# Row sums by accumulating DMAs among the heads, and another order of transfers and units around the gate's stage, in a hybrid attention trunk on one core

## The chip, the core and the metric

The kernel runs on one core of a Trainium2 chip. The core has five engines, each with its own in-order queue: TensorE (PE in the profile, with its weight loads as PEld), VectorE (DVE), ScalarE (ACT), GpSimd (POOL) and SyncE (SP), which only issues DMAs. POOL issues DMAs too; in this kernel those that add to what lies in memory are issued by POOL. All transfers run on the core's 16 DMA engines. The metric is the device time of one launch in microseconds (us); the median of three runs counts.

## The reference

One layer of a decoder trunk on 1024 tokens of width 2048, all in f32. Shortened:

```python
hn = rmsnorm(h, norm_mix_g)
sb_q, sb_k, sb_v, sb_g, df_q, df_k, df_v, df_g = split(hn @ w_in)      # 8 x 1024 columns
sb_out = stick_breaking_attention(sb_q, sb_k, sb_v)                    # 8 heads of 128
df_out = rmsnorm(differential_attention(rope(df_q), rope(df_k), df_v, lam), subln_g)   # 8 heads of 128
mixed = concat([sb_out * silu(sb_g), df_out * silu(df_g)])
h = h + mixed @ w_out
gate = sigmoid(rmsnorm(h, norm_ple_g) @ w_ple_gate)
h = h + gate * (p @ w_ple_proj)                                        # p: 1024 x 256
return rmsnorm(h, norm_final_g)
```

## The kernel before, in words

**Tiles.** Everything is kept transposed: a tile has 128 features as partitions and a half of the tokens (`HALF` = 512) along the free axis. Half 1 holds the later 512 tokens and is worked on first, then half 0. Each f32 operand of a product is split into a high and a low part, and a product is three matmuls: high by high (L213), high by low (L214) and low by high (L215). A `unit` is 96 such matmuls of 128x512 that give two feature blocks of 128; it takes its weights from `Stream` in four chunks of 512 KB. For each chunk SP loads `wraw` (L150), ACT makes `whi` (L151), DVE makes `wlo` (L152).

**Stages.** First come the 16 heads for half 1 (the trace's first 800 us): eight stick-breaking heads (0 to 7), then eight differential ones (8 to 15). Then come the 16 heads for half 0 (to about 1750 us): `ORDER0` begins with the differential heads 8 to 15 and ends with the stick-breaking ones. A head is two units and, interleaved with the matmuls of the next units by `Side`, its attention. At its end DVE has the gated result of the head, `sg`, and SP stores it to `mixed_d` in memory (L410). For half 0 POOL loads the keys and values of half 1 back (`k2`, `kl`, `v2`, L571 to L575). The sum of squares of half 0's input, which half 0's norm needs, is taken at head 8 of half 1: sixteen tiles `xs` are loaded (SP, L585), squared (ACT, L109) and added (POOL, L110), all at once.

**The out-projection** is one level of a Strassen-like scheme (seven products in place of eight). Its four quadrants are A11, A12 (half 1) and A21, A22 (half 0); each product works on a quadrant or on a sum of quadrants: S1 = A21 + A22, S2 = S1 - A11, S3 = A21 - A11, S4 = A12 - S2. `combine` makes these sums for a pair of heads, eight times: SP loads four tiles `cmb` (L246), POOL does four additions of 128x512 (L249 to L252), and SP stores four tiles to `comb_d` (L254). It is called among the heads of half 0, and the last time inside the out-projection. The products then run for 16 pairs (ph, u). Each gets its result tile `hc` from DVE, and POOL puts it to memory: a plain store to `half_d` in ph 0, an accumulating DMA into `h_d` in ph 1 (`put`, L744 and L746). In this stage the order on DVE and ACT is the order in the code (`manual_schedule`).

**The gate's stage** (from about 2060 us) begins with the last pair (1, 7) of the out-projection. Loads of the normalised operand (`xl`, L910 to L914), of the embedding (`praw`, which gives `ph` and `pl`, L655 to L657) and of its weights (`pw`, giving `pwh` and `pwl`, L665 to L669) stand between the last products, whose results are `hc` of L939 and L993. Then come eight gate units for half 1 and eight for half 0. The first two are held back, `acc0` in `acc` banks and `acc1` in a `za` tile, until the norm's `rstd` is there, which needs the sixteen tiles of the residual loaded (`load_h`) and squared; these stand in one burst behind the first unit. `ple` (12 matmuls, L677 to L679) multiplies the embedding by `pwh` and `pwl` into `pls`; `gated` multiplies by the gate and adds. For unit u from 2 on the order is `ple(1, u)`, `plew(1, u + 1)`, unit, `gated(1, u)`. There is one `ph` and one `pl`, rewritten for half 0 by `embedding(0)`; this stands behind `ple(1, 7)` and ahead of the last unit of half 1.

**The tail.** The last unit of half 0 is done in two quarters of 256 tokens (`tq`). Behind each, DVE does the gate (L1116 to L1119), a square (L1121), PE sums it over the partitions (`ssps`, L1122), `rstd_from` (L90 to L94) gives `r`, and `final` multiplies the tiles by it (L623, L626) and SP stores the output. POOL does the multiplications for tq 0 and the first ones for tq 1.

Of the kernel before, what the change touches and what calls it, by code (L numbers as in the profile page):

```python
# [13 lines left out]
F32 = mybir.dt.float32  # L14
# [6 lines left out]
P = 128  # L21
# [7 lines left out]
ORDER1 = [*range(16)]  # L29
ORDER0 = [*range(8, 16), 0, 4, 1, 5, 2, 6, 3, 7]  # L30
EPS = 1e-6
# [15 lines left out]
def _body(ctx, nc, tc, ap):  # L47
# [95 lines left out]

    def wprep(wsrc, pc, by_halves=False):
        raw = wp.tile([P, 2, 2, 2, P], F32, name="wraw", tag="wraw", bufs=2)
        hi = wp.tile([P, 2, 2, 2, P], F32R, name="whi", tag="whi")
        lo = wp.tile([P, 2, 2, 2, P], F32R, name="wlo", tag="wlo")

        def part(o):
            lastw[0] = nc.sync.dma_start(raw[:, o], wsrc[pc][:, o])  # L150
            A.copy(hi[:, o], raw[:, o])  # L151
            V.tensor_tensor(lo[:, o], raw[:, o], hi[:, o].bitcast(F32), op=ALU.subtract)  # L152

        part(slice(0, 1 if by_halves else 2))
        return hi, lo, partial(part, slice(1, 2))

    class Stream:
# [6 lines left out]
        def gates(self):  # L164
            units = [ap["w_gate"][u] for _ in range(2) for u in range(8)]
            self.todo = deque((w, pc) for w in units[:-1] for pc in range(4))
            self.prep()

        def prep(self, by_halves=False):
            hi, lo, second = wprep(*self.todo.popleft(), by_halves=by_halves)  # L170
            self.ready.append((hi, lo))
            return second
# [58 lines left out]

    def combine(ph, i):

        a, b = KA[ph][i]
        if lastput[0] is not None:
            with tc.issue_after(lastput[0].ins):
                return combine_(ph, i, a, b)
        return combine_(ph, i, a, b)

    lastput = [None]  # L240

    def combine_(ph, i, a, b):
        t = []
        for src in (mixed_d[0, a], mixed_d[0, b], mixed_d[1, a], mixed_d[1, b]):
            x = ev.tile([P, HALF], F32, name="cmb", tag="xt", bufs=4)
            nc.sync.dma_start(x, src)  # L246
            t.append(x)
        a21, a22, a11, a12 = t
        G.tensor_tensor(a22, a21, a22, op=ALU.add)  # L249
        G.tensor_tensor(a21, a21, a11, op=ALU.subtract)  # L250
        G.tensor_tensor(a11, a22, a11, op=ALU.subtract)
        G.tensor_tensor(a12, a12, a11, op=ALU.subtract)  # L252
        for j, x in enumerate((a22, a11, a21, a12)):
            nc.sync.dma_start(comb_d[ph, j, i], x)  # L254


    def attention(at, pz, half, hd, q, qz, K, KL, VV, sg, vf):
# [102 lines left out]
        def mix(pr, g):  # L360
# [25 lines left out]
            if sb:  # L386
                V.tensor_tensor(sg[:, ms_], av, sg[:, ms_], op=ALU.mult)
                if pr == 1:
                    nc.sync.dma_start(mixed_d[half, hd], sg)
                return  # L390
# [9 lines left out]
        def norm(pr):  # L400
# [8 lines left out]
            if pr == 1:  # L409
                nc.sync.dma_start(mixed_d[half, hd], sg)  # L410

# [22 lines left out]
    with tc.tile_pool(name="at", bufs=2) as at, tc.tile_pool(name="pz", bufs=2, space=PSUM) as pz:  # L434
# [4 lines left out]
        for half in (1, 0):  # L439
# [34 lines left out]
            for hd in (ORDER0, ORDER1)[half]:  # L474
# [103 lines left out]
                side.add(attention(at, pz, half, hd, q, qz, K, KL, VV, sg, vf))  # L578
                if half == 1 and hd == H:
                    pin = lastw[0].ins  # L580
                    ss0 = SumSq(ev, "ssq")
# [12 lines left out]
                if half == 0 and hd < H and hd:  # L594
                    n = ORDER0.index(hd) - H
                    combine(*((0, n - 1) if n < 5 else (1, n - 5)))

# [53 lines left out]

        def embedding(half):
            for k in range(2):
                praw = ev.tile([P, HALF], F32, name="praw", tag="xt", bufs=4)
                nc.sync.dma_start(praw, ap["pT"][k * P:(k + 1) * P, half * HALF:half * HALF + HALF])  # L655
                A.copy(ph[:, k, :], praw)
                V.tensor_tensor(pl[:, k, :], praw, ph[:, k, :].bitcast(F32), op=ALU.subtract)  # L657
# [3 lines left out]
        plws = {}  # L661

        def plew(half, u):
            wr = ev.tile([P, 2, 2, P], F32, name="pw", tag="xt", bufs=4)
            nc.sync.dma_start(wr, ap["w_pp"][u])  # L665
            wh = at.tile([P, 2, 2, P], F32R, name="pwh", tag="awh")
            wl = at.tile([P, 2, 2, P], F32R, name="pwl", tag="awl")
            A.copy(wh, wr)
            V.tensor_tensor(wl, wr, wh.bitcast(F32), op=ALU.subtract)  # L669
            plws[half, u] = wh, wl  # L670

        def ple(half, u):
            wh, wl = plws.pop((half, u))
            z = pz.tile([P, 2, HALF], F32, name="ple", tag="z")
            for c in range(2):
                for k in range(2):
                    T.matmul(z[:, c, :], wh[:, k, c, :], ph[:, k, :], start=k == 0, stop=False)  # L677
                    T.matmul(z[:, c, :], wh[:, k, c, :], pl[:, k, :], start=False, stop=False)
                    T.matmul(z[:, c, :], wl[:, k, c, :], ph[:, k, :], start=False, stop=k == 1)  # L679
            pls = pair("pls", "st")  # L680
            A.copy(pls, z)
# [59 lines left out]
        def put(o, ph, hf, ch):  # L741

            if ph:
                lastput[0] = G.dma_start(h_d[hf, ch], o, accum_op=ALU.add)  # L744
            else:
                lastput[0] = G.dma_start(half_d[hf, ch], o)  # L746

# [106 lines left out]
        def whigh():  # L854
# [8 lines left out]
            else:  # L863
                t = at.tile([P, 2, 4 * P], F32R, name="wpr", tag=tag, bufs=BUFS.get(tag, 2))
            A.copy(t[:, 0], src)  # L865
            wmade.append((src, t))

        def wlow():
# [6 lines left out]
            wmade[i] = None  # L875
            V.tensor_tensor(t[:, 1], src, t[:, 0].bitcast(F32), op=ALU.subtract)
            ph, u = UNITS[n]
# [64 lines left out]
        for ph in range(2):  # L942
            for u in range(8):
                last = ph == 1 and u == 7
                r = {}
                for e in ((1, u), (1, u + 8), (0, u), (0, u + 8)) if ph else ():
                    r[e] = ev.tile([P, HALF], F32, name="hr", tag="xt", bufs=4)
                    nc.sync.dma_start(r[e], half_d[e])
# [17 lines left out]
                if ph:  # L966
                    V.tensor_tensor(u2, u2, r[1, u + 8], op=ALU.add)

                def p2():
# [25 lines left out]
                if ph:  # L995
                    V.tensor_tensor(s1, s1, r[0, u], op=ALU.add)
                if last:
                    p2()
                prev = u, ph, b, c, s1, u2
                if ph == 0 and u == 1:  # L1000
                    combine(1, 3)
                if ph == 0 and 1 <= u < 5:
# [3 lines left out]
        pl = pair("pl", "v", F32R)  # L1006
        embedding(1)
# [6 lines left out]
        while xq and len(xq) > 8:  # L1014
            xq.popleft()[1]()

        last_ = [None, None]
        X = GX
        ple(1, 0)
        ple(1, 1)  # L1020
        for _ in range(len(xq) - 4):
            xq.popleft()[1]()
        plew(1, 2)
        s2 = SumSq(ev, "ssq")

        def xrest():
            while xq:
                xq.popleft()[1]()

        acc0 = unit(X, mid={2: xrest})  # L1030
        man2.__exit__(None, None, None)
        ss1 = SumSq(ev, "rstd1")
        for u in range(8):
            load_h(1, u)
            for c in range(2):
                ss1.add(h[1, u + 8 * c])
        za = pz.tile([P, 2, HALF], F32, name="za", tag="z")
        rs = []
        acc1 = unit(X, acc=[za[:, 0, :], za[:, 1, :]], mid={3: lambda: rs.append(ss1.rstd(ev, "rstd0"))})
        rstd = rs[0]  # L1040
        ss0 = SumSq(ev, "rstd1")
        gated(1, 0, acc0, rstd)
        gated(1, 1, acc1, rstd)
        for u in range(2, 8):
            ple(1, u)
            if u < 7:
                plew(1, u + 1)
            else:
                embedding(0)
                plew(0, 0)  # L1050
            acc = unit(X)
            for v in ((0, 1), (2, 3), (4,), (5,), (6,), (7,))[u - 2]:
                load_h(0, v)
# [45 lines left out]
        for tq in range(2):  # L1099
# [13 lines left out]
            for c in range(2):  # L1113
# [7 lines left out]
                V.tensor_tensor(s, t, t, op=ALU.mult)  # L1121
# [65 lines left out]
```

## Time and profile before

| | us |
|---|---|
| runs | 2513.76, 2515.78, 2515.96 (median 2515.78) |
| profiled execution, time | 2510.27 |
| profiled execution, span | 2508.5 |
| PE busy | 2441.4 (97%) |
| DVE, ACT, POOL busy | 1668.4, 1161.9, 288.9 |

A span is the time from the first to the last instruction of the profiled execution. In a window of 50 us PE is busy all 50.00 us where nothing holds it up. Matmuls overlap: each row of a 128x512 matmul is 0.39 us long, while the next starts 0.23 us later, so a stall that the profile shows as x us of idle time costs x + 0.16 us. A granted clock below 1.00 is a stretch in which TensorE ran slower.

### The profile page before, as it was taken

The numbers are of one execution on the slowest core, as the hardware profiler recorded it, in microseconds if no ns is written. First come the engines' busy times: TensorE is split into PE (matmuls) and PEld (weight loads), VectorE is DVE, ScalarE is ACT, GpSimd is POOL, SyncE is SP. The second block draws the span as 40 slices with busy tenths as digits, with TensorE's granted clock in tenths as the row PEclk, the third lists the DMA queues.
The fourth block names the chain that finished last, engine by engine and source line by source line (L and its number), as shares of the span: only waits on it lengthen the run. The fifth ranks groups of instructions, "written<-read, shape, count | busy, mean of one in ns | idle before, by whom it ended". The sixth has DMA issues, their size and how long they took to land.

```text
span 2508.5 us, 31234 instructions
## 1 busy us (share of the span) xinstructions
PE 2441.4 (97%) x11626; PEld 2034.8 (81%) x11626; DVE 1668.4 (67%) x2677; ACT 1161.9 (46%) x1920; POOL 288.9 (12%) x281
## 2 busy tenths in 40 slices
PE   8999999999999999999999999999999998999996
PEld 7888888788887888888887888887787876888886
DVE  6554555777877888888876565667678673547555
ACT  6332333555556655555555333335523224637342
POOL 3000000300000000001111010101021114321112
PEclk9999999999999999999999999999999999999998
DMA  5333333633334333334443333435656786333433
GB/s 189 113 116 116 114 105 125 206 123 118 109 122 164 121 107 122 114 117 143 148 142 126 101 126 94 135 113 183 228 190 217 164 199 211 129 119 115 133 101 101
DMA packets 135415, 346.26 MB, mean 138 GB/s; under 512 B 14496, under 2 KB 18592, under 8 KB 135264
## 3 DMA queue, kind: packets, MB, share of 16 engines
q1 hardware_dynamic: 114096, 288.43, 35.6%
q0 software_dynamic: 21168, 55.85, 7.8%
q8 instruction: 91, 1.49, 0.2%
q14 instruction: 60, 0.49, 0.1%
HBM read 281.31 MB, written 71.30 MB: 141 GB/s over the span
## 4 chain that ended last, share of the span: by engine, by line
PE 87%; DVE 7%; DMA 2%; ACT 2%; issue 1%; SPq 0%; DVEq 0%; ACTq 0%
PE acc L213 20%; PE acc L214 20%; PE acc L215 20%; PE tp L345 2%; PE pbc L756 2%; PE pbc L758 2%; PE pbc L757 2%; DVE st L306 1%; PE z L286 1%; PE z L287 1%; PE av L378 1%; DVE wlo L152 1%; PE av L377 1%; PE av L376 1%; PE pa L758 1%
## 5 line engine op out<-in xcount | busy, mean ns | idle before, releaser
L213 PE MATMUL acc<-xh,whi 128*128 128x512 f32 x2464 | 981.4, 398 | 6.3 <-ACT xh L138 6.3
L214 PE MATMUL acc<-xl,whi 128*128 128x512 f32 x2464 | 963.9, 391 | 0.8 <-DVE xl L139 0.8
L215 PE MATMUL acc<-xh,wlo 128*128 128x512 f32 x2464 | 964.0, 391 | 0.0
L152 DVE TENSOR_TENSOR wlo<-wraw,whi 128x1024 fp32r<-128x1024 f32 (+1 forms) x317 | 398.8, 1258 | 374.5 <-ACT whi L151 369.2
L215 PEld LDWEIGHTS acc<-xh,wlo 128*128 128x128 f32 x2464 | 463.6, 188 | 101.1 <-DVE wlo L152 1.3
L151 ACT CAST whi<-wraw 128x1024 fp32r<-128x1024 f32 (+1 forms) x317 | 333.0, 1051 | 457.2 <-PE acc L214 397.0
L213 PEld LDWEIGHTS acc<-xh,whi 128*128 128x128 f32 x2464 | 464.8, 189 | 93.6 <-ACT xh L138 6.8
L214 PEld LDWEIGHTS acc<-xl,whi 128*128 128x128 f32 x2464 | 464.9, 189 | 88.3 <-DVE xl L139 2.3
L357 ACT CAST awh<-tp 128x256 fp32r<-128x256 f32 (+1 forms) x160 | 80.3, 502 | 180.9 <-PE tp L345 153.5
L358 DVE TENSOR_TENSOR awl<-tp,awh 128x256 fp32r<-128x256 f32 (+1 forms) x160 | 93.1, 582 | 97.9 <-ACT awh L357 96.7
L110 POOL TENSOR_TENSOR ssq<-ssq,sq 128x512 f32<-128x512 f32 x80 | 119.0, 1488 | 326.6 <-ACT sq L109 278.8
L314 ACT ACTIVATE et<-z,mx 128x512 f32<-128x512 f32 (+7 forms) x128 | 94.6, 739 | 53.6 <-DVE mx L311 52.7
L865 ACT CAST wpr<-T 128x512 fp32r<-128x512 f32 x64 | 39.2, 623 | 164.9 <-DVE T L822 164.0
L306 DVE TENSOR_TENSOR_SCAN st<-pt 128x511 f32<-128x511 f32 (+3 forms) x64 | 89.9, 1405 | 20.8 <-ACT pt L304 20.2
L311 DVE TENSOR_REDUCE mx<-z 128x1 f32<-128x512 f32 (+7 forms) x128 | 96.4, 753 | 1.2
L304 ACT ACTIVATE pt<-z 128x512 f32<-128x512 f32 (+3 forms) x64 | 41.6, 650 | 79.7 <-DVE z L293 79.7
L378 PE MATMUL av<-awl,v 128*128 128x256 f32 x256 | 73.4, 287 | 5.2 <-DVE awl L358 5.2
L376 PE MATMUL av<-awh,v 128*128 128x256 f32 x256 | 72.5, 283 | 0.7 <-ACT awh L357 0.7
L377 PE MATMUL av<-awh,v 128*128 128x256 f32 x256 | 72.3, 283 | 0.0
L286 PE MATMUL z<-k,q 128*128 128x512 f32 (+2 forms) x160 | 56.9, 360 | 4.5 <-ACT et L314 4.5
L322 DVE SCALAR_TENSOR_TENSOR et<-et,l 128x512 f32<-128x512 f32 (+3 forms) x64 | 53.0, 829 | 11.8 <-ACT et L321 11.8
L321 ACT ACTIVATE et<-et,l 128x512 f32<-128x512 f32 (+3 forms) x64 | 49.7, 777 | 17.6 <-DVE l L320 17.1
(309 smaller groups left out, 3627.8 us busy)
## 6 DMA issues: line engine op xcount, KB each, us to landing
wraw<-w_in SPq DMA_DIRECT2D x255, 512.0 KB, 3.6
wraw<-w_gate SPq DMA_DIRECT2D x64, 512.0 KB, 3.6
wraw<-w_out SPq DMA_DIRECT2D x56, 256.0 KB, 3.7
k_d<-k POOLq DMA_DIRECT2D x16, 512.0 KB, 3.9
v_d<-v POOLq DMA_DIRECT2D x16, 512.0 KB, 2.9
mixed_d<-sg SPq DMA_DIRECT2D x32, 256.0 KB, 3.1
k<-k_d POOLq DMA_DIRECT2D x16, 512.0 KB, 3.6
v<-v_d POOLq DMA_DIRECT2D x16, 512.0 KB, 4.4
```

The source lines that it names most:

```text
L110: lastadd[0] = eng.tensor_tensor(self.acc, self.acc, s, op=ALU.add)
L151: A.copy(hi[:, o], raw[:, o])
L152: V.tensor_tensor(lo[:, o], raw[:, o], hi[:, o].bitcast(F32), op=ALU.subtract)
L213: T.matmul(acc[c], hi[:, k2, kh, c, :], xh, start=first, stop=False)
L214: T.matmul(acc[c], hi[:, k2, kh, c, :], xl, start=False, stop=False)
L215: T.matmul(acc[c], lo[:, k2, kh, c, :], xh, start=False, stop=last)
L306: V.tensor_tensor_scan(st[:, off + 1:nkey], pt[:, off:nkey - 1], pt[:, off:nkey - 1], initial=1.0, op0=ALU.mult, op1=ALU.bypass)
L311: V.reduce_max(mx, z[:, vw], axis=AX.X, negate=True)
L314: A.activation(et[:, vw], z[:, vw], AF.Exp, bias=mx[:, 0:1], accum_out=l)
L376: T.matmul(av, vv[:, 0, blk % 4, :], wh, start=blk == 2 * pr + 1, stop=False)
L377: T.matmul(av, vv[:, 1, blk % 4, :], wh, start=False, stop=False)
L378: T.matmul(av, vv[:, 0, blk % 4, :], wl, start=False, stop=last)
```

## The change

1. `combine` is gone. `mixed`, called where a head's result was stored, makes the sums as the heads finish. For half 1 ACT makes a negated copy `neg`; heads 0 to 3 and 8 to 11 store it (SP) as the start of S2, S3 and S4, and heads 4 to 7 and 12 to 15 add it to S4 by an accumulating DMA (POOL). For half 0 each head issues three DMAs on POOL that add its result to sums, and heads 0 to 3 and 8 to 11 store it as the start of S1 (SP). S4 is kept negated, and its weights are negated as they are made. Not stored to `mixed_d` any more: half 0's heads 0 to 3 and 8 to 11. `ORDER0` has heads 0 to 7 in plain order.
2. The sixteen `xs` tiles are loaded and squared four at a time in heads 1 to 4 of half 1.
3. Before the gate's stage: `praw` of half 1 is loaded ahead of the last pair, `pw` of units 0 to 2 within it; the first gate weights are loaded there too, and split behind the A22 product; the order of the four `hr` loads of a pair is changed. The residual is loaded and squared two tiles at a time over the chunks of the first units, and a third unit (`zb`) runs before the first `gated`.
4. For units 3 to 7 of half 1 the order is unit, `ple(1, u)`, `plew(1, u + 1)` (or `embedding(0)`), `gated(1, u)`.
5. In the tail DVE does all multiplications of `final`; those of tq 0 stand inside tq 1, behind its square, and `rstd_from` has a higher priority.

```diff
-    def combine_(ph, i, a, b):
-        t = []
-        for src in (mixed_d[0, a], mixed_d[0, b], mixed_d[1, a], mixed_d[1, b]):
-            x = ev.tile([P, HALF], F32, name="cmb", tag="xt", bufs=4)
-            nc.sync.dma_start(x, src)
...
+    def mixed(half, hd, t):
+        ph, second, i = (0 if hd >= H else 1), hd % H >= 4, hd % 4
+        S1, S2, S3, S4 = [comb_d[ph, j, i] for j in range(4)]
+        if half == 1 or second:
+            nc.sync.dma_start(mixed_d[half, hd], t)
+        if half == 1:
+            n = ev.tile([P, HALF], F32, name="neg", tag="xt", bufs=4)
+            A.activation(n, t, AF.Copy, scale=-1.0)
+            if second:
+                G.dma_start(S4, n, accum_op=ALU.add)
+            else:
+                for d in (S2, S3, S4):
+                    nc.sync.dma_start(d, n)
+            return
+        if second:
+            G.dma_start(S1, t, accum_op=ALU.add)
+        else:
+            nc.sync.dma_start(S1, t)
+            G.dma_start(S3, t, accum_op=ALU.add)
+        G.dma_start(S2, t, accum_op=ALU.add)
+        G.dma_start(S4, t, accum_op=ALU.add)
...
-                if half == 1 and hd == H:
+                if half == 1 and 1 <= hd < 5:
...
-                    for kt in range(NK):
+                    for kt in range(4 * hd - 4, 4 * hd):
...
+                if last:
+                    embedding_load(1, (("rstd0", 1), ("rstd1", 1)))
...
+        embedding()
         plew(1, 0)
-        stream.gates()
         rest_of(prev, True)
+        gate0()
         plew(1, 1)
...
+        acc0 = unit(X, mid={2: xrest, 3: partial(residual, 0)})
+        za = pz.tile([P, 2, HALF], F32, name="za", tag="z")
+        acc1 = unit(X, acc=[za[:, 0, :], za[:, 1, :]], mid={i: partial(residual, i + 1) for i in range(4)})
...
+        zb = pz.tile([P, 2, HALF], F32, name="zb", tag="z")
...
+        acc2 = unit(X, acc=[zb[:, 0, :], zb[:, 1, :]], mid={0: partial(residual, 5), 1: more, 3: norm1})
...
-        for u in range(2, 8):
+        gated(1, 2, acc2, rstd)
+        for u in range(3, 8):
+            acc = unit(X)
             ple(1, u)
             if u < 7:
                 plew(1, u + 1)
             else:
-                embedding(0)
+                embedding_load(0, (("xt", 4), ("xt", 4)))
+                embedding()
                 plew(0, 0)
-            acc = unit(X)
...
+            if tq:
+                final(0, slice(0, Q), r2, range(8))
...
-            rstd_from(ms, 1.0 / NK, eps6, EPS, r2, r3)
-            if tq == 0:
-                final(0, ts, r2, range(8), eng=G)
-            else:
-                final(0, ts, r2, (0, 1, 2), eng=G)
-                final(0, ts, r2, (3, 7, 4, 5, 6))
+            with tc.high_priority(offset=400):
+                rstd_from(ms, 1.0 / NK, eps6, EPS, r2, r3)
+        final(0, ts, r2, range(8))
```

More of the change, by code (lines that the diff above doesn't have):

```diff
@@ L650, in load_h, with embedding_load, embedding @@
                 h[half, u + 8 * c] = hc[c]
-        def embedding(half):
+        praws = []
+        def embedding_load(half, tags):
             for k in range(2):
-                praw = ev.tile([P, HALF], F32, name="praw", tag="xt", bufs=4)
+                praw = ev.tile([P, HALF], F32, name="praw", tag=tags[k][0], bufs=tags[k][1])
                 nc.sync.dma_start(praw, ap["pT"][k * P:(k + 1) * P, half * HALF:half * HALF + HALF])
+                praws.append(praw)
+        def embedding():
+            for k in range(2):
+                praw = praws.pop(0)
                 A.copy(ph[:, k, :], praw)
@@ L661, in _body, with plew_load @@
         plws = {}
+        pws = {}
+        def plew_load(half, u):
+            pws[half, u] = ev.tile([P, 2, 2, P], F32, name="pw", tag="xt", bufs=4)
+            nc.sync.dma_start(pws[half, u], ap["w_pp"][u])
         def plew(half, u):
[L664 to L665 removed]
+            if (half, u) not in pws:
+                plew_load(half, u)
+            wr = pws.pop((half, u))
             wh = at.tile([P, 2, 2, P], F32R, name="pwh", tag="awh")
@@ L679, in ple @@
                     T.matmul(z[:, c, :], wl[:, k, c, :], ph[:, k, :], start=False, stop=k == 1)
-            pls = pair("pls", "st")
+            pls = pair("pls", "pt" if half == 1 and u == 2 else "st")
             A.copy(pls, z)
@@ L743, in put @@
             if ph:
-                lastput[0] = G.dma_start(h_d[hf, ch], o, accum_op=ALU.add)
+                G.dma_start(h_d[hf, ch], o, accum_op=ALU.add)
             else:
-                lastput[0] = G.dma_start(half_d[hf, ch], o)
+                G.dma_start(half_d[hf, ch], o)
         def ftile():
```

94 lines of the change are left out of this document (48 added, 46 removed).

## The prediction, made before the changed kernel was run

> **What bounds the kernel now.** I read the page first, then PE's waits, then a table of windows of 50 us, and then the rows around each window in which PE lost time.
>
> ```profile
> PE 2441.4 (97%) x11626; PEld 2034.8 (81%) x11626; DVE 1668.4 (67%) x2677; ACT 1161.9 (46%) x1920; POOL 288.9 (12%) x281
> ```
>
> PE is the bound, 97% busy. The change leaves the matmuls what they were, so only the 67 us in which PE is idle, and slow stretches of its clock, can be won. The windows (columns: window, its length, busy time of PE, PEld, DVE, ACT and POOL, granted clock, DMA share, GB/s) show where these lie:
>
> ```profile
> 100.00:150.00 50.00, 50.00 (x239) 41.88 (x238) 25.48 (x39) 15.86 (x27) 1.23 (x2) 1.00 0.36 111
> 450.00:500.00 50.00, 46.53 (x218) 38.61 (x217) 37.96 (x77) 30.25 (x57) 14.49 (x14) 0.97 0.54 174
> 800.00:850.00 50.00, 47.95 (x217) 39.26 (x216) 40.76 (x86) 29.55 (x59) 1.07 (x2) 0.95 0.46 145
> 1450.00:1500.00 50.00, 47.88 (x233) 39.46 (x233) 33.55 (x39) 18.27 (x28) 10.70 (x6) 1.00 0.42 137
> 1500.00:1550.00 50.00, 50.00 (x256) 42.52 (x256) 31.70 (x39) 19.73 (x28) 1.06 (x2) 1.00 0.33 106
> 2000.00:2050.00 50.00, 50.00 (x222) 41.26 (x221) 32.46 (x51) 10.85 (x19) 8.62 (x10) 1.00 0.74 161
> 2050.00:2100.00 50.00, 42.34 (x179) 34.33 (x178) 33.13 (x49) 22.46 (x34) 6.02 (x7) 0.93 0.86 242
> 2100.00:2150.00 50.00, 47.44 (x199) 38.10 (x199) 22.72 (x24) 30.31 (x43) 25.27 (x18) 0.97 0.45 158
> 2250.00:2300.00 50.00, 50.00 (x220) 41.02 (x220) 35.31 (x44) 34.12 (x49) 8.82 (x6) 1.00 0.36 117
> ```
>
> What PE waited for in three stretches, the first of 1180 to 1280 us and the second of 1460 to 1720, the rest from the whole run (us in total, times, longest):
>
> ```profile
> PE av L378 <- DVE awl L358: 1.9, 2, 0.9
> PE tp L345 <- DVE et L322: 1.2, 2, 0.6
> ...
> PE av L373 <- DVE lead L351: 4.7, 3, 1.6
> PE av L378 <- DVE awl L358: 1.7, 3, 0.6
> ...
> PE pbc L756 <- DVE hc L939: 5.8, 1, 5.8
> PE z L286 <- ACT et L314: 4.5, 2, 3.5
> PE pbc L756 <- DVE hc L993: 2.5, 2, 1.8
> PE za L215 <- DVE wlo L152: 1.5, 1, 1.5
> PE za L213 <- ACT whi L151: 1.1, 1, 1.1
> ```
>
> A stall costs its idle time and 0.16 us more, since rows of matmuls overlap.
>
> **1. Row sums.** Heads with `combine` stall PE, the one between them (1500 to 1550) doesn't. Its POOL additions slow DVE: the same scan and the same difference of a head without `combine` (1405) and one with it (1462):
>
> ```profile
> 1405.32 2.02 DVE L306 TENSOR_TENSOR_SCAN st<-pt 128x895 f32<-128x895 f32 x1
> 1407.44 1.09 DVE L307 TENSOR_TENSOR bt<-st,bt 128x895 f32<-128x895 f32 x1
> ...
> 1462.62 3.11 DVE L306 TENSOR_TENSOR_SCAN st<-pt 128x895 f32<-128x895 f32 x1
> 1463.93 2.88 POOL L251 TENSOR_TENSOR cmb<-cmb 128x512 f32<-128x512 f32 x1
> 1465.84 1.93 DVE L307 TENSOR_TENSOR bt<-st,bt 128x895 f32<-128x895 f32 x1
> ```
>
> That is 1.93 us late on DVE by two instructions, about the 1.6 us of the longest wait for `lead`. The waits of both stretches add up to 1.9 + 1.2 + 4.7 + 1.7 = 9.5 us in 10 waits, so 9.5 + 10 x 0.16 = 11.1 us. All of it goes if POOL does no additions there. What comes instead: 56 accumulating DMAs on POOL; on SP 96 DMAs (32 stores of `sg`, 32 loads, 32 stores of sums) become 56; 16 negated copies on ACT; 32 weight operations with a sign, in place of as many without, at nothing. The nearest rows for an accumulating DMA:
>
> ```profile
> h_d<-hc POOLq DMA_DIRECT2D x32, 256.0 KB, 5.1
> half_d<-hc POOLq DMA_DIRECT2D x32, 256.0 KB, 3.5
> ...
> 2062.47 0.86 POOL L744 DMA_DIRECT2D h_d<-hc  x1 [6.33 <-DVE hc L939]
> 2062.68 0.69 DVE L876 TENSOR_TENSOR wpr<-b,wpr 128x512 fp32r<-128x512 f32 x1
> ```
>
> It lands after 5.1 us, keeps POOL for 0.86 us, and DVE beside it takes its usual 0.69. Three per head of some 58 us are at most 3 x 5.1 = 15 us of all DMA engines, 0.26 of the head on top of 0.33; the window from 2000 ran at 0.74, with such DMAs, and lost nothing. On POOL's queue they stand behind the `k2` and `v2` loads of the next head and half a head ahead of those after it. The copy `neg` is some 0.6 us of an ACT that is 0.3 to 0.6 busy. It stands where SP's store waited for the same `sg`. In these places I take 0; the lower end, no gain at all, is where each collides with weight loads; the upper is 13, with the DVE time of the other `combine`s. Taken: -11 (range -13 to 0).
>
> **2. Squares of half 0's input.** The 3.5 us wait of `z` L286 lies at 453, in the window from 450. ACT stood there for the sixteen tiles and for POOL's additions:
>
> ```profile
> ACT sq L109 <- DMA xs<-xT: 4.7, 4, 1.7
> ACT sq L109 <- POOL ssq L110: 1.0, 3, 0.4
> ```
>
> The stall costs 3.5 + 0.16, and the clock of 0.97 another 0.03 x 50 = 1.5 us: 5.1. In heads 1 to 4 each four tiles meet an ACT that is busy for 16 of 50 us and a DVE for 25 (the window from 100); the price there is between 0 and 1 us.  Taken: -4.5 (range -5 to 0).
>
> **3. Entry to the gate.** The two windows from 2050 lost 7.66 + 2.56 idle and, by their clocks, 3.5 + 1.5 us, 15.9 us with 4 x 0.16. DVE and ACT in order show why `hc` L939 is late, though its product was done:
>
> ```profile
> ACT ph L656 <- DMA praw<-pT: 5.7, 1, 5.7
> ACT pwh L668 <- DMA pw<-w_pp: 2.3, 1, 2.3
> ...
> DVE pwl L669 <- ACT pwh L668: 2.2, 1, 2.2
> DVE pl L657 <- ACT ph L656: 1.4, 1, 1.4
> ```
>
> With `praw` and `pw` loaded early both waits on DMA go, and with them 2.2 + 1.4 + the cast's own time on DVE. I follow DVE's order in the changed kernel: `pl` and `pwl` are still ahead of the addition of L939, so some 1.0 of the 5.8 us stays. The 1.8 us of L993 stays, as the work ahead of it is the same. The waits for `whi` and `wlo` (1.1 and 1.5) came from the burst of squares; with two squares to a chunk of 5.45 us they go. New: the third unit needs the banks of the norm's sum and of `acc` at once; DVE frees them 7.4 us after the sum by my count of its queue, PE arrives after 6.1, so 1.3 us. Left over: 1.8 + 1.0 + 1.3, 3 x 0.16 and some 1 us of clock, 5.6. Taken: -10 (range -14, if only L993 stays, to -2, if the loads, which SP issues one after the other, are late again).
>
> **4. Units 3 to 7.** Here something is lost. `ple(1, 7)` now runs behind the last unit of half 1, and only then may `ph` and `pl` be overwritten; `ple(0, 0)` is the very next on PE. Before, this cast was done 22 us earlier, and the window from 2250 lost nothing:
>
> ```profile
> 2262.45 0.61 ACT L656 CAST ph<-praw 128x512 fp32r<-128x512 f32 x1
> ...
> 2287.34 1.28 ACT L1073 ACT_TABLE_LOAD   x1
> 2289.18 0.60 ACT L668 CAST pwh<-pw 128x512 fp32r<-128x512 f32 x1
> 2289.68 1.01 ACT L681 COPY pls<-ple 128x1024 f32<-128x1024 f32 x1
> ```
>
> From the end of `ple(1, 7)` at about 2287.0: ACT loads its table until 2288.6, then come `ph` of the first half (0.6), `pwh` (0.6), `pls` (1.0) and `ph` of the second (0.6), 2291.4. DVE has `pl`, `pwl`, two products of `gated` that wait for `pls`, 0.69 each, and the second `pl` is there at 2292.9. The fifth matmul of `ple(0, 0)` needs it and would have run at 2287.9: +5.0. In pieces, as the first matmuls go as their parts come. For the clock I take the 0.03 x 50 = 1.5 us of the window from 450, which had a stall of this size; the window from 800 (0.95) shows that pieces slow it as well. Taken: +6 (range +3, if the table load comes earlier, to +8).
>
> TensorE: Matmul & The Clock Gate, section "The HAM clock gate", a page of the Trainium skill, has the clock halve only after about 3.4 us without work. By it a stall in pieces shorter than that costs no clock, and this term would be +5.0; the row of the window from 800 speaks against it, as its 2.05 us of idle time went with a clock of 0.95.
>
> **5. Tail.** Without POOL's `final` DVE is fast again:
>
> ```profile
> 2490.74 1.37 DVE L1121 TENSOR_TENSOR sq<-h 128x256 f32<-128x256 f32 x1
> 2494.84 0.42 DVE L93 SCALAR_TENSOR_TENSOR r<-r,r 128x256 f32<-128x256 f32 x1
> ```
>
> L1119 and L1121 fall from about 1.4 to 0.42 each, four times, 3.9 us; but seven products of tq 0 at 0.69 and two at 0.42 (5.7 us) now stand on DVE in the same stretch, some of it in waits for ACT. Counted through the queue, `r` comes 1.1 us earlier and the last product 1.8 earlier, and a store follows each as before. Taken: -1.8 (range -4 to +1).
>
> **Sum.** -11 - 4.5 - 10 + 6 - 1.8 = -21.3. Against the profiled execution, 2510.27, that gives 2489.0; the median of the runs is 5.5 us (0.22%) above it, so 2494.5. A measurement can tell about 0.2%, 5 us, from no change.
>
> **Rivals.**
> - A, the forecast: 2494.5, its own range 2485 to 2503. Chance 0.57.
> - B, DVE's stalls among the heads stay, since they come of the long scans and not of POOL, or the entry to the gate is late through another load. Without term 1, or without 3: 2504 to 2506. Against it stands the scan of 2.02 against 3.11 us. Chance 0.18.
> - C, slower: the accumulating DMAs delay the weights. Each of the 16 heads of half 0 issues three, one behind the other, and each is 1.6 us longer under way than a plain store from POOL (5.1 against 3.5). If the weight chunk beside them lands later by what the second and third take more, 3.2 us, and PE stands for it, the 16 heads lose 51 us and the kernel takes 2546. It decides from (21.3 + 5)/16 = 1.6 us a head, just the price of one. Against it: the window from 2000, with such DMAs at a share of 0.74 and PE busy for 50.00. Chance 0.12.
> - D, the new stall of term 4 is covered, as ACT's casts go earlier than I count, and L993 goes too: 2494.5 - 6 - 2 = 2486 or a little less. Chance 0.08.
> - E, the gains and the new stalls cancel (gate -2, heads -5): 2511 to 2520. Chance 0.05.
>
> DMA: Bandwidth & Descriptors, section "Why small descriptors are slow (HBM only)", of the Trainium skill, speaks for C: it has each small packet carry a fixed overhead, 27% at 256 bytes. By that figure I estimate 3.5 x 1.27 = 4.4 us for an accumulating DMA, if its packets are that small; the 5.1 measured is above it, and no row here shows what such DMAs cost others.
>
> **From these:** the range is 2481 to 2514, which leaves out C and part of D and E. Faster by over 0.2% (below 2511): A, B and D, 0.83. Within 0.2%: most of E, 0.04. Slower: C and the rest, 0.13.
>
> **What would show it.** Right: windows 1150 to 1300 and 1450 to 1750 with PE at 50.00 and DVE's scan at 2.02; no wait of `z` L286 at 453; the wait for L939's `hc` near 1; a wait of `ple` for `ph` and `pl` of some 5 us near 2265; the tail's L1121 at 0.42. Wrong: waits for weights among the heads of half 0 or `k2` loads that land late (C); waits for `awl` and `lead` as before (B); a stall after the norm's sum much above 1.3 us, which would take the gate's gain.

## The result and the profile after

The changed kernel takes 2493.89 us as the median of four runs (2490.08 to 2496.32), the kernel before 2514.77 us: a ratio of 0.991, with a 95% interval of 0.9896 to 0.9924. Predicted were 2494.5 us. The profiled execution took 2490.08 us, its span is 2488.2 us, 20.3 us less than before; the sum of the prediction was -21.3.

Windows of 50 us of the changed kernel, with the columns of the prediction's table (everything behind 1200 lies up to 25 us earlier than before):

```profile
450.00:500.00 50.00, 50.00 (x240) 41.86 (x239) 37.07 (x81) 27.18 (x52) 2.83 (x5) 1.00 0.42 135
...
1450.00:1500.00 50.00, 50.00 (x258) 42.48 (x256) 28.62 (x37) 18.30 (x28) 3.77 (x5) 1.00 0.30 93
...
1750.00:1800.00 50.00, 46.84 (x237) 39.17 (x235) 24.25 (x36) 21.90 (x39) 5.94 (x9) 1.00 0.76 249
1800.00:1850.00 50.00, 48.88 (x202) 39.84 (x203) 34.94 (x55) 13.51 (x24) 5.42 (x10) 0.93 0.49 162
...
2050.00:2100.00 50.00, 47.41 (x208) 38.58 (x207) 26.06 (x35) 23.62 (x34) 8.54 (x8) 1.00 0.80 243
2100.00:2150.00 50.00, 48.49 (x213) 39.46 (x211) 23.25 (x26) 27.41 (x38) 20.50 (x14) 1.00 0.37 120
...
2250.00:2300.00 50.00, 46.65 (x184) 35.61 (x183) 28.21 (x36) 29.32 (x40) 2.92 (x2) 0.93 0.35 110
```

The squares' window (450) is full, and so are those of the heads of half 0 from 1150 to 1300 and from 1350 to 1700, the one from 1450 among them. The one from 1300, at the change from the differential to the stick-breaking heads, lost 3.58 us, as much as there before (1.52 + 2.06 us in two windows). The out-projection now begins in the window from 1700, some 20 us earlier than before. The gate's entry lost 2.59 + 1.51 us in place of 7.66 + 2.56, at full clock. Two windows are worse than before: in the one from 1800 the clock is 0.93 (it was 1.00), and the one from 2250, which was full, lost 3.35 us and has a clock of 0.93 too. PE's waits in the changed kernel, longest in total first:

```profile
PE ple L696 <- ACT ph L668: 2.7, 1, 2.7
PE ssps L1169 <- DVE sq L1168: 2.6, 2, 1.5
PE pbc L775 <- DVE hc L1022: 2.5, 2, 1.8
...
PE pbc L777 <- DVE wpr L901: 1.6, 2, 1.1
...
PE pbc L775 <- ACT wpr L887: 1.5, 1, 1.5
PE acc L220 <- DVE gt L708: 1.5, 1, 1.5
...
PE pbc L775 <- DVE hc L964: 0.8, 1, 0.8
...
PE ple L697 <- DVE pl L669: 0.6, 1, 0.6
```

L964 is the old L939, L1022 the old L993, L1168 the old L1121. The waits for `hc` L964 (0.8), for `gt` L708 in front of unit 3 (1.5) and for `ph` and `pl` (2.7 and 0.6) stand where the prediction put them. The one for `wpr` of L887, near 1800, it did not have.

Both kernels were traced a second time. The table gives the time between the same matmuls in both, counted by their number, in us. In the changed kernel the stage of the last pair holds one `ple` less (twelve matmuls, 2.7 us) and the change of halves in the gate's stage one more; the last column takes that out.

| stage | before, two traces | after, two traces | difference of the means |
|---|---|---|---|
| start | 54.1, 55.8 | 56.2, 55.6 | +0.9 |
| head 8 of half 1 | 83.5, 83.5 | 78.2, 79.8 | -4.5 |
| last heads of half 1, change to half 0 | 86.5, 86.1 | 82.7, 83.6 | -3.1 |
| heads of half 0 with `combine` | 650.1, 651.0 | 636.4, 635.8 | -14.5 |
| out-projection, ph 0 | 182.0, 185.3 | 190.4, 192.7 | +7.9 |
| last pair and first three gate units | 102.4, 102.8 | 90.1, 90.0 | -12.5, without the moved `ple` -9.8 |
| change of halves in the gate's stage | 52.5, 52.5 | 62.2, 63.1 | +10.2, without the moved `ple` +7.5 |
| tail | 22.5, 22.5 | 16.8, 17.4 | -5.4 |

The total came out as forecast, but part of that is luck: the out-projection lost 7.9 us that no term of the sum held, and the heads, the tail and the change from half 1 to half 0 won some 10 us more than their terms.

### The profile page after: what moved, and what is told of

Its sections match the earlier page's. It is cut to its first block, busy times and chain, and to the rows that moved or that the text cites. A ratio compares the mean times of both kernels' runs of the same rounds, so it can differ in the third digit from the quotient of the medians.

```text
span 2488.2 us, 31261 instructions
## 1 busy us (share of the span) xinstructions
PE 2440.0 (98%) x11626; PEld 2035.9 (82%) x11626; DVE 1637.2 (66%) x2687; ACT 1168.7 (47%) x1936; POOL 264.8 (11%) x295
## 2 busy tenths in 40 slices
DMA packets 137720, 350.46 MB, mean 141 GB/s; under 512 B 14752, under 2 KB 18848, under 8 KB 137568
## 3 DMA queue, kind: packets, MB, share of 16 engines
q0 software_dynamic: 29232, 70.53, 11.8%
## 4 chain that ended last, share of the span: by engine, by line
PE 91%; DVE 4%; ACT 2%; DMA 2%; issue 1%; SPq 0%; DVEq 0%; ACTq 0%
PE acc L220 21%; PE acc L221 21%; PE acc L222 21%; PE tp L352 2%; PE pbc L777 2%; PE pbc L775 2%; PE pbc L776 2%; PE z L294 1%; PE z L293 1%; PE av L385 1%; PE av L384 1%; PE av L383 1%; PE pa L777 1%; PE pa L776 1%; PE pa L775 1%
## 5 line engine op out<-in xcount | busy, mean ns | idle before, releaser
L220 PE MATMUL acc<-xh,whi 128*128 128x512 f32 x2432 | 968.5, 398 | 7.8 <-ACT xh L138 6.3
L221 PE MATMUL acc<-xl,whi 128*128 128x512 f32 x2432 | 950.9, 391 | 0.4 <-DVE xl L139 0.4
L222 PE MATMUL acc<-xh,wlo 128*128 128x512 f32 x2432 | 950.8, 391 | 0.0
L222 PEld LDWEIGHTS acc<-xh,wlo 128*128 128x128 f32 x2432 | 457.4, 188 | 98.6
L220 PEld LDWEIGHTS acc<-xh,whi 128*128 128x128 f32 x2432 | 458.2, 188 | 94.6 <-ACT xh L138 6.9
L221 PEld LDWEIGHTS acc<-xl,whi 128*128 128x128 f32 x2432 | 458.6, 189 | 86.1 <-DVE xl L139 1.8
L365 DVE TENSOR_TENSOR awl<-tp,awh 128x256 fp32r<-128x256 f32 (+1 forms) x160 | 93.1, 582 | 102.8 <-ACT awh L364 101.6
L321 ACT ACTIVATE et<-z,mx 128x512 f32<-128x512 f32 (+7 forms) x128 | 94.5, 738 | 55.6 <-DVE mx L318 55.0
L887 ACT CAST wpr<-T 128x512 fp32r<-128x512 f32 x64 | 39.1, 621 | 171.0 <-DVE T L841 170.1
L294 PE MATMUL z<-kl,qz 128*128 128x512 f32 (+2 forms) x160 | 57.5, 359 | 0.0
```

Of the source, the lines that this page charges most:

```text
L220: T.matmul(acc[c], hi[:, k2, kh, c, :], xh, start=first, stop=False)
L221: T.matmul(acc[c], hi[:, k2, kh, c, :], xl, start=False, stop=False)
L222: T.matmul(acc[c], lo[:, k2, kh, c, :], xh, start=False, stop=last)
L321: A.activation(et[:, vw], z[:, vw], AF.Exp, bias=mx[:, 0:1], accum_out=l)
L365: V.tensor_tensor(wl[:, o, :], tp[:, o, :], wh[:, o, :].bitcast(F32), op=ALU.subtract)
```

## The experiments

**The changed kernel and the kernel before, once more.** No edit.

> The changed kernel once more, for a second trace. In the first trace three stretches moved that the prediction had no term for: the first unit (+2.1 us), the change from half 1 to half 0 near 810 us (-4.0) and the first half of the out-projection, from its first product to the end of its pairs of ph 0 (+8.4). Theory (they come of the edit): each is there again within 1 us. Rival (chance in one execution): they move by 2 us or more. The median is expected between 2490 and 2497.

> The kernel before once more, for a second trace. Theory (the three stretches come of the edit): each as long as in the first trace of before, within 1 us. Rival (chance): one or more differ by 2 us.

2493.26 us (median of four) and 2516.02 us (one run). The traces are the second ones of the table. The change from half 1 to half 0 and the out-projection differ between the kernels by more than between traces of one (0.4 to 0.9 and 2.3 to 3.3 us), so they come of the edit; for the out-projection that holds of a part only, as the run without the last head's DMAs shows. The start doesn't: before took 54.1 and 55.8.

**The sums on POOL again,** with all that goes with them: the loads and stores on SP, the old order of the heads, no negated copies and no negated weights.

```diff
-                    mixed(half, hd, sg)
+                    nc.sync.dma_start(mixed_d[half, hd], sg)
...
+                if half == 0 and hd < H and hd:
+                    n = ORDER0.index(hd) - H
+                    combine(*((0, n - 1) if n < 5 else (1, n - 5)))
```

> The changed kernel with the old combine (POOL additions, loads and stores on SP, the old order of heads) and all else as changed. Theory: DVE beside POOL's additions is slow again, the scan of 895 goes from 2.02 to about 3.1 us, and the five groups of stalls among the heads of half 0 return, 13.5 us; the out-projection gets back the 8.4 us that the accumulating DMAs of its first pairs cost it, so the kernel is only some 5 us slower than the changed one. Rival (the 8.4 us have another cause): 13 us slower. Rival (the stalls come of the order of heads or of the loads on SP, as likely to return): cannot be told by this run alone, the scan's time tells it.

2501.45 us (2499.26 to 2504.59; ratio to before 0.9951, 0.9935 to 0.9968), 8 us slower than the changed kernel. The heads took 651.8 us (15.4 more), the out-projection's first half 182.8 (7.6 less). The scan and the difference over 895 columns, of all eight heads, in the groups of the kernel before, of the changed kernel and of this one (busy us, mean ns):

```profile
L306 DVE TENSOR_TENSOR_SCAN st<-pt 128x895 f32<-128x895 f32 x8 | 19.4, 2429 | 1.0 <-ACT pt L304 1.0
L307 DVE TENSOR_TENSOR bt<-st,bt 128x895 f32<-128x895 f32 x8 | 11.2, 1405 | 0.8
```

```profile
L313 DVE TENSOR_TENSOR_SCAN st<-pt 128x895 f32<-128x895 f32 x8 | 16.1, 2015 | 1.0 <-ACT pt L311 1.0
L314 DVE TENSOR_TENSOR bt<-st,bt 128x895 f32<-128x895 f32 x8 | 8.7, 1092 | 0.8
```

```profile
L313 DVE TENSOR_TENSOR_SCAN st<-pt 128x895 f32<-128x895 f32 x8 | 19.4, 2428 | 1.0 <-ACT pt L311 1.0
L314 DVE TENSOR_TENSOR bt<-st,bt 128x895 f32<-128x895 f32 x8 | 11.2, 1405 | 0.8
```

With POOL's additions the means are the old ones to a nanosecond. Three of the eight scans take 3.1 us and the other five 2.0, before as here; in the changed kernel all eight take 2.0. The order of the heads was put back with the sums, so this run doesn't part the two, but the slow instructions are those beside POOL. The prediction's step 1 holds for the heads; and the edit that won there is the one that lost in the out-projection.

**Without the last head's three accumulating DMAs** (its result is then missing from the sums).

```diff
+        if hd == 7:
+            return
         if second:
             G.dma_start(S1, t, accum_op=ALU.add)
```

> The changed kernel without the three accumulating DMAs of the last head (head 7 of half 0, whose result is left out of S1, S2 and S4), which POOL issues inside the out-projection. Theory (these three hold up the weights of w_out beside them, which landed after 7.9 us in place of 4.5): the stalls of PE on the weights of L887 and L901 near 1800 go, 3.0 us, and with them the slow clock of that stretch; 5 us faster than the changed kernel, between 3 and 8. Rival (the weights are late for other reasons, or the clock is slow anyway): no change within 1.5 us.

2486.19 us (2484.07 to 2491.07), 7 us faster than the changed kernel; the first half of the out-projection took 184.6 us in place of 190.4 and 192.7. First the changed kernel's timeline (start, length, engine, what it waited for): POOL starts the three within 1.1 us, and the weights that SP asked for at 1789.85 land 7.9 us later and hold DVE and PE up.

```profile
1785.97 0.88 POOL L256 DMA_DIRECT2D comb_d<-sg  x1 [9.26 <-DVE sg L394]
...
1789.85 0.98 SPq L835 DMA_DIRECT2D wraw<-w_out  x1
...
1797.88 0.69 DVE L841 TENSOR_TENSOR T<-wraw 128x512 f32<-128x512 f32 x1 [5.27 <-DMA wraw<-w_out]
...
1800.00 0.50 PE L775 MATMUL pbc<-cS2h,wpr 128*128 128x512 f32 x1 [1.54 <-ACT wpr L887]
```

The DMA issues of ten us around that place (KB each, median us to landing), in the kernel before, where three loads of `combine` stood, and in the changed one:

```profile
cA12l<-mixed_d SPq DMA_DIRECT2D x4, 256.0 KB, 5.4
wraw<-w_out SPq DMA_DIRECT2D x3, 256.0 KB, 5.6
cmb<-mixed_d SPq DMA_DIRECT2D x3, 256.0 KB, 5.0
```

```profile
cA12l<-mixed_d SPq DMA_DIRECT2D x4, 256.0 KB, 7.2
comb_d<-sg POOLq DMA_DIRECT2D x3, 256.0 KB, 6.7
wraw<-w_out SPq DMA_DIRECT2D x3, 256.0 KB, 6.5
```

And PE's waits from 1780 to 1830 without the three:

```profile
PE pbc L777 <- DVE u L994: 1.6, 1, 1.6
PE pbc L779 <- DVE wpr L903: 0.4, 1, 0.4
```

The wait for L887 is gone and the one for the weights' low part is 0.4 in place of 1.1; the clock from 1800 is 1.00, where the changed kernel has 0.64 and 0.50:

```profile
1800.00:1804.00 4.00, 2.88 (x7) 2.06 (x8) 3.46 (x6) 1.51 (x3) 0.00 (x0) 0.64 0.15 53
1804.00:1808.00 4.00, 4.00 (x11) 3.04 (x11) 2.22 (x4) 1.15 (x2) 0.54 (x1) 0.50 0.43 133
```

The stretch that this touches is short. From PE's matmul number 8660 to 8720 (1797 to 1817 us) it took 14.3 us without the three, 13.9 and 14.3 in the kernel before, and 17.2 to 20.6 us, 19.3 in the mean, in the seven traces that have the three as the changed kernel has them (its own two and those of five variants below). So the three DMAs cost some 5 us: about 2.4 as stalls, and the rest as the slow clock behind them (0.36 x 4 + 0.50 x 4 = 3.4 us in this trace).

The other 2.7 of the 7.9 us lie ahead of them, from matmul 8380 to 8480 (1734 to 1759 us): 25.1 to 28.4 us in the seven traces, 23.1 without the three, 22.9 and 25.2 in the two traces of the kernel before. There PE waits for one `hc`: 1.5 us in the first trace of before and 2.0 us in the second, and the ten microseconds around it (first trace, then second) have another clock, the third number from the end:

```profile
1765.00:1775.00 10.00, 9.23 (x50) 7.96 (x51) 3.46 (x6) 3.18 (x6) 0.55 (x1) 1.00 0.59 211
1765.00:1775.00 10.00, 7.09 (x27) 5.66 (x28) 5.69 (x7) 4.86 (x9) 1.12 (x2) 0.83 0.51 184
```

This part comes and goes in one and the same kernel, so what of it is the edit's is not shown.

**All sums as plain stores** (the sums are then not made).

```diff
-            G.dma_start(S1, t, accum_op=ALU.add)
+            G.dma_start(S1, t)
...
```

> The changed kernel with the 56 accumulating DMAs as plain stores from POOL (the sums are then not made). Theory a (adding in memory is what makes them slow): comb_d<-sg lands in some 4 us in place of 7.3, and the first half of the out-projection falls from 190.4 to 192.7 us to 186 or less. Theory b (three transfers of 256 KB at once are enough): it stays above 189. Among the heads no change by either, since PE stood nowhere there.

One run, 2487.32 us; the first half of the out-projection took 187.4 us, between the two theories. `comb_d<-sg` landed after 4.2 us in place of 7.3. From matmul 8660 to 8720 it took 15.7 us, against 14.3 without the three and 17.2 to 20.6 with them: by this one trace most of the cost there is that the DMAs add, and a smaller part that three transfers are there at all. What else is over in the 187.4 us lies from 8380 to 8480 (26.2 us). Among the heads PE stood nowhere that it had not stood before.

**The last head's sums later,** one each behind pairs 2, 3 and 4, from memory to memory.

```diff
+        if hd == 7:
+            return
...
+                if ph == 0 and 2 <= u < 5:
+                    with tc.issue_after(lastput[0].ins):
+                        G.dma_start(comb_d[1, (0, 1, 3)[u - 2], 3], mixed_d[0, 7], accum_op=ALU.add, max_dma_last_dim=512)
```

> The changed kernel with the three accumulating DMAs of the last head issued behind pairs 2, 3 and 4 of ph 0, one each, from memory (mixed_d) to memory (comb_d). Theory (what hurt was three at once beside the weights of the first pairs): the first half of the out-projection takes some 185 us as without them, and the kernel is 5 to 7 us faster than the changed one. Rival (each delays the weights beside it wherever it stands): 188 or more.

2490.26 us (2488.47 to 2491.19), 3 us faster; the stretch took 187.1 us, where 185 was expected. From matmul 8660 to 8720 it took 14.3 us, as without the three, and where they now stand, up to 9140, nothing stands out (97.0 us against 95.8 to 97.7 in the other traces). What was over lies from 8380 to 8480 again (26.1 us), ahead of them. So the theory holds at its place: apart from each other they cost nothing that this trace shows.

**The squares of half 0's input at head 8 again.**

```diff
-                if half == 1 and 1 <= hd < 5:
+                if half == 1 and hd == H:
...
```

> The changed kernel with the sixteen loads, squares and additions back at head 8 of half 1. Theory: the wait of z for et near 453 returns with 3.5 us and its slow clock, the stretch of head 8 takes 83.5 us again in place of 78.2, 5.3 us more; nothing in heads 1 to 4. A second question, open so far: the change from half 1 to half 0 became 3 to 4 us shorter (82.7 and 83.6 against 86.5 and 86.1 us) without a term in the prediction. Theory a: the squares' place did it (buffers of the tag xt or POOL freer there); then it is back at 86 here. Theory b: another part did; then it stays at 83.

One run, 2498.47 us. The stretch of head 8 took 86.0 us, 6 to 8 more, and PE's waits from 440 to 500 are

```profile
PE z L293 <- ACT et L321: 3.9, 1, 3.9
PE acc L220 <- DVE vf L559: 0.8, 1, 0.8
```

The wait is back, and the stretch is even 2.5 us longer than in the kernel before (83.5): these waits are 4.7 us where it had 3.5, and the clock from 450 is 0.93 where it had 0.97. The change from half 1 to half 0 stayed at 83.0, so theory b: it isn't the squares' place.

**praw and pw loaded late again.**

```diff
-                if last:
-                    embedding_load(1, (("rstd0", 1), ("rstd1", 1)))
...
+        embedding_load(1, (("xt", 4), ("xt", 4)))
         embedding()
```

> The changed kernel with praw and pw loaded where they were, right ahead of their casts. Theory: DVE waits for them again in front of the addition of L939, PE's wait for its hc goes from 0.8 to about 5.8 us, and the entry to the gate takes some 6 us more than the changed kernel's 90.1 (with the clock 8). Rival (the early loads were worth nothing, the burst of squares did it): within 1.5 us of 90.1. The change from half 1 to half 0 is not touched.

One run, 2501.68 us; the entry took 98.0 us in place of 90.1, 7.9 more. PE's waits from 2030 to 2150:

```profile
PE pbc L775 <- DVE hc L964: 6.0, 1, 6.0
PE pbc L775 <- DVE hc L1018: 1.8, 1, 1.8
```

The old wait of 5.8 is there, at 6.0 in place of 0.8; the rest is clock (0.93 in the window from 2050, in place of 1.00). Most of step 3's gain hangs on these loads.

**The residual in one burst again.**

```diff
-        acc0 = unit(X, mid={2: xrest, 3: partial(residual, 0)})
+        acc0 = unit(X, mid={2: xrest})
+        man2.__exit__(None, None, None)
+        for u in range(9):
+            residual(u)
...
```

> The changed kernel with the residual loaded and squared in one burst behind the first gate unit, as before, and the third unit ahead of the first gated as now. Theory: the waits for whi and wlo in the second unit return, 2.6 us idle and 1.5 us of clock, the entry to the gate takes 3 to 5 us more than 90.1. Rival (the third unit and the early loads make up for it): within 1.5 us.

One run, 2494.44 us; the entry took 93.8 us, 3.7 more. PE's waits from 2030 to 2150:

```profile
PE acc L220 <- DVE gt L708: 1.5, 1, 1.5
...
PE za L222 <- DVE wlo L151: 1.5, 1, 1.5
...
PE za L220 <- ACT whi L150: 0.3, 1, 0.3
```

The wait for `wlo` is back with its 1.5, that for `whi` with 0.3, where the kernel before had 1.1. The wait for `gt` in front of unit 3 is there either way, so it belongs to the third unit, as predicted.

**POOL's multiplications in the tail again.**

```diff
-            if tq:
-                final(0, slice(0, Q), r2, range(8))
...
+            if tq == 0:
+                final(0, ts, r2, range(8), eng=G)
...
```

> The changed kernel with the tail as before: POOL multiplies tq 0 and the first of tq 1. The changed tail was 16.8 to 17.4 us against 22.45, 5.3 us shorter where 1.8 was predicted. Theory: all of it is this edit: 22.4 us here. Rival (half of it comes with stores or a DVE that are freer for other reasons): 19 to 21.

One run, 2500.97 us; the tail took 22.5 us, as before. All of the 5.4 us is this edit, which also takes back the higher priority of `rstd_from`; the two were not parted. The timelines of this kernel and of the changed one:

```profile
2479.92 1.37 DVE L1166 TENSOR_TENSOR h<-h,gt 128x256 f32<-128x256 f32 x1
2481.32 1.37 DVE L1168 TENSOR_TENSOR sq<-h 128x256 f32<-128x256 f32 x1
```

```profile
2467.44 3.09 DVE L631 TENSOR_TENSOR h<-h,r 128x512 f32<-128x512 f32 x5
...
2472.78 0.41 DVE L1168 TENSOR_TENSOR sq<-h 128x256 f32<-128x256 f32 x1
...
2478.48 4.30 DVE L631 TENSOR_TENSOR h<-h,r 128x512 f32<-128x512 f32 x7
```

**The old order for unit 7 of half 1 alone.**

```diff
-            acc = unit(X)
+            if u < 7:
+                acc = unit(X)
             ple(1, u)
...
                 plew(0, 0)
+                acc = unit(X)
```

> The changed kernel with the old order for unit 7 of half 1 alone: ple(1, 7), embedding(0) and plew(0, 0) ahead of the unit. Theory: the wait of ple(0, 0) for ph and pl goes with its slow clock; the stretch of the change inside the gate's stage takes 52.5 us again in place of 62.2 to 63.2, and the kernel is 9.7 us faster, 2484. Rival (the bank or buffer that ple(1, 7) then needs is still held by gated(1, 6), or the casts delay the weights): a stall of 1 to 4 us in unit 7, and only 6 us faster.

2487.30 us (2484.00 to 2491.27; ratio to before 0.9889, 0.9874 to 0.9904). The stretch takes 52.5 us again, and PE waits for nothing from 2230 to 2300. It is only 6 to 7 us faster than the changed kernel: 2.7 of the 9.7 us was the moved `ple`, which now stands in the stage ahead (100.7 in place of 98.0 us). The expectation had counted it as a loss. What it got rid of, in the changed kernel's timeline:

```profile
2262.42 0.39 PE L698 MATMUL ple<-ph,pwl 128*128 128x512 f32 x1
...
2263.58 1.28 ACT L1120 ACT_TABLE_LOAD   x1
2264.88 0.62 ACT L668 CAST ph<-praw 128x512 fp32r<-128x512 f32 x1
...
2265.55 0.80 PE L696 MATMUL ple<-ph,pwh 128*128 128x512 f32 x1 [2.73 <-ACT ph L668]
...
2268.17 0.69 DVE L669 TENSOR_TENSOR pl<-praw,ph 128x512 fp32r<-128x512 f32 x1
...
2268.91 0.80 PE L697 MATMUL ple<-pl,pwh 128*128 128x512 f32 x1 [0.62 <-DVE pl L669]
2269.50 0.63 PE L698 MATMUL ple<-ph,pwl 128*128 128x512 f32 x1
```

The first row is the end of `ple(1, 7)`, at 2262.8. Then come the table load and `ph`, and 6.0 us behind the first row's end the second `pl` is done, at 2268.9: the chain that the prediction counted, with 5.9. The matmuls behind the stall are 0.63 to 0.80 us long in place of 0.39; the granted clock was 0.67 from 2264 to 2268 and 0.50 from there to 2272.

**Both mends,** the old order for unit 7 and the last head's sums later.

> The changed kernel with both: the old order for unit 7 and the last head's sums later. Theory: the two add up, 9.7 + 6, so 2478 as a median and a ratio of 0.985 to the kernel before. Rival (one of them only moves a stall): 2484 to 2488.

2481.78 us (2478.02 to 2485.71): a ratio to before of 0.9867 (0.985 to 0.9883), 12 us below the changed kernel. Alone the two had won 6 to 7 and 3 us; together they win a little more than the sum, within the spread of the runs. It is less than the expected 2478, since each had been priced too high. It is the fastest version here.

## Why the prediction was right, and where it wasn't

1. **Row sums.** The mechanism is as told: POOL's additions made DVE late, and without them the stalls are gone. The gain was 14.5 us, against 11 taken and a bound of 13, so outside the term's range; it was mis-sized because it summed waits. A stick-breaking head with `combine` became 3.2 us shorter, while its two waits had been 1.6 and 0.6 us idle; the rest lies in hesitations of 0.2 us and less around them, which no wait shows. The cost of the DMAs that came instead was taken as nothing. Among the heads that holds: PE was busy for 50.00 us in all windows there but the one from 1300, which stalled as before, though `comb_d<-sg` needed 7.3 us to land, not the 5.1 of the nearest row, as three stand one behind the other. It fails at one place. The last head ends inside the out-projection, where SP loads weights and operands at a DMA share of 0.76 to 0.86, and there the three cost some 5 us. This is rival C's mechanism, at one head in place of sixteen. The row that was to speak against it, the window from 2000 with a share of 0.74, has its accumulating DMAs one by one, 2.7 us apart or more; three at once beside weights that are due is another case. The overhead of small packets in the Trainium skill's DMA: Bandwidth & Descriptors, section "Why small descriptors are slow (HBM only)", doesn't explain them: the page gives 27% for packets of 256 bytes (3 of 11 cycles, so the prediction's estimate should have been 3.5 x 11/8 = 4.8 us), and the trace has no more packets under 2 KB with accumulating DMAs than with plain stores (18848 in both). What differs is that each of the 56 DMAs is 64 packets more (29232 against 25648 on that queue), none of the added ones under 2 KB. With plain stores of the same bytes most of the loss at that place went, by one trace.
2. **Squares.** -4.5 predicted, -4.5 measured; the wait returns when they are put back. Nothing to speak of was lost in heads 1 to 4 (0.2 us between the first traces).
3. **Entry to the gate.** -10 predicted, -9.8 measured. The leftovers by name: L993's 1.8 (1.8), L939's 1.0 (0.8), the new wait in front of unit 3 1.3 (1.5). Putting the loads back costs 7.9 us, putting the burst back 3.7: together 11.6, a little more than the stage won, since the third unit's wait isn't undone by either.
4. **Units 3 to 7.** +6 predicted, +7.5 measured between the traces, 7.0 to 7.9 by the mend (62.2 and 63.1 less 52.5 and the moved 2.7). The stall's chain is right. Split another way than told: 2.7 + 0.6 us idle and the rest as slow matmuls, at a clock of 0.93 over 50 us, 3.5 us. The prediction had 5.0 and 1.5; the longest single wait was 2.7 us. By the Trainium skill's TensorE: Matmul & The Clock Gate, section "The HAM clock gate", a wait shorter than 3.4 us would cost no clock, and the term would have been 5.0; the measured 7 us and the clock speak against that rule at this place, as the window from 800 did.
5. **Tail.** -1.8 predicted, -5.4 measured: the largest miss of size, outside its own range of -4 to +1. Counted from the first `gt` of tq 0, `r` came 2.6 us earlier (1.1 predicted) and the last product 3.9 (1.8 predicted): the products of tq 0 took 0.62 us each in a row, not 0.69, and five of them were done before PE came to the sum over the partitions. "A store follows each as before" was wrong: before, DVE and POOL made the last products side by side, so that the last five stores left SP within 2.1 us, the last landing 5.2 us behind the last product; now one goes out each 0.6 us and the last lands after 3.5.

Two stretches moved without a term. Of the out-projection's 7.9 us some 5 are the last head's three DMAs; the rest, ahead of them, is open. The change from half 1 to half 0 became 3.1 us shorter, in both traces and in each variant. PE's wait for `et` there is 1.8 in place of 3.3 us; ACT waits for the fifth `xt` tile, which lands 3.3 us after its issue in place of 5.1, beside the 512 KB of `cs` that POOL asks for at the same moment. Of the five parts only the first two act before this place. Each put back alone leaves the stretch at 83.4 and 83.0 us; both together were not tried, so what shifts the two transfers stays open.

The rivals: B is refuted by the sums on POOL and by the 9.8 us that the entry won, D by the wait for `ph`, E by the total (its own figures, gate -2 and heads -5 with the other terms as they were, give 2508.5 us, not 2511 to 2520). C as a whole is refuted, its mechanism isn't.

## What to carry to other kernels

A transfer that costs nothing in one stage is priced for each stage in which it is issued: list where its last instances fall, and look at the DMA share and the weights due there. When a producer is moved behind the work that used to cover it (here the cast of the next half's embedding behind the last unit), the single buffer between the two halves becomes the stall; moving that one step back was worth 6 us. Work moved between stages is taken out before stages are compared. And a stretch that differs between two traces of one kernel is looked at piece by piece before its whole difference is put down to an edit.

## What was not expected of the hardware

Three accumulating DMAs issued together landed after 7.3 us in the median, single ones to `h_d` after 5.1, plain stores in their place after 4.2; the one issue of weights 2.8 us behind the last head's three landed after 7.9. With a stall of 2.7 us and smaller ones behind it the clock was 0.67 from 2264 to 2268 and 0.50 up to 2272 (matmuls of 0.63 to 0.80 us in place of 0.39), some 3.4 us, so the clock cost as much as the stalls themselves. The wait for one `hc` at the start of the out-projection was 1.4 to 1.7 us in three of the fourteen traces here, with a clock of 1.00 over ten microseconds from its end, and 1.9 to 2.0 us in the other eleven, with 0.66 or 0.83. The slowing of DVE beside POOL's additions of two tiles is sharp: 2015 against 2429 ns for the mean of eight scans, of which three had POOL beside them, and the same to a nanosecond when the additions were put back.
